# Layer B's memory projection moved into layer A's last pair, and queries projected in halves

## The chip, the cores and the metric

One core of a Trainium2 chip runs the whole kernel. The metric is the device time of one execution in microseconds (us); lower is better. The engines are named as in the profile: PE is TensorE (matmuls), PEld its weight loads, DVE is VectorE, ACT is ScalarE, POOL is GpSimd, SP is SyncE, which issues all DMAs of this kernel.

## What is computed

An encoder of two layers over 1024 tokens of width 1024. Layer A (index 0) uses windowed attention with 12 query heads and 4 key/value heads, layer B (index 1) neighbourhood attention on a 16 x 64 grid with 12 heads. In each layer 4 more heads attend to a memory of 256 rows. Cut to what matters here:

```python
for i in range(DEPTH):                      # DEPTH = 2
    h = rms_norm(x, norm_mix_pre[i])
    m = rms_norm(mem, norm_mem[i])
    mkv = einsum('bmd,de->bme', m, w_mem_kv[i])    # memory keys and values, 256 x 512
    mk, mv = mkv[..., :256], mkv[..., 256:]
    proj = einsum('bsd,de->bse', h, w_in[i])       # queries, keys, values, memory queries
    tok = windowed_gqa(...) if i % 2 == 0 else neighbourhood_attn(...)
    mem_out = memory_attn(qm, mk, mv)
    x = x + rms_norm(concat(tok, mem_out) @ w_out[i], norm_mix_post[i])
    gu = rms_norm(x, norm_ffn_pre[i]) @ w_gu[i]
    x = x + rms_norm((silu(gate) * up) @ w_down[i], norm_ffn_post[i])
```

Memory keys and values of layer B depend on `mem` and on weights alone, so they can be computed at any time before layer B's memory heads.

## The kernel before

Every float32 product is made of three matmuls: each operand is split into a high part (an ACT copy to fp32r) and a low part (a DVE or POOL subtraction), and `mm3` (L91 to L93) adds high x high, high x low and low x high. A weight unit of 128 x 1024 is loaded by `load_raw` (L105, tile `wr`, two buffers) and split by `split_raw` (L115, L116, tiles `wh` and `wl`, three buffers).

**The opening** (L585 on) projects layer A's first values while the rows of x are normed and transposed. Then, for each layer c, it projects key unit c of layer A: the first half (512 tokens) of it, then four transposes of the normed memory rows (L186, split into tiles `mT` by L97 and L98), then the second half, and then that layer's memory keys and values (`memory_kv`): two units of 24 matmuls with 256 columns and two passes of 24 over two units. Layer A's results stay on the chip, but for its second key unit; that one and all of layer B's go to DRAM (`mem_scr`) and are loaded back later (`mem_back`: in layer A with the start of pair 1).

**The attention of a layer** runs over eight pairs of heads in the order 0, 6, 1, 7, 2, 3, 4, 5 (6 and 7 are the memory pairs). A pair has 16 units (8 blocks of 128 tokens, two heads). `heads` writes PE's order by hand: the scores of unit k (L254, L255, tile `pss`), then some matmuls of a filler, then the drains: the transposes of unit k-3 (L282, `pst`) and the weighted values of unit k-5 (L292, `psv`). The filler of a pair is the projection of what the next pair needs, spread evenly over the 16 units; the last pair has none. A query unit (`q_item`) is two halves of 512 tokens, 24 matmuls each into a tile `psg`. Units 0 to 7 of a pair read the first half's tile, units 8 to 15 the second's. The first pair's queries are projected ahead of the pairs.

**A query tile** (`q_tiles`) holds high and low parts of two heads, interleaved over the partitions. In layer A ACT writes the high part (L208), DVE the low part into `ql` (L209, one buffer), and three DMA moves of 64 x 512 (L201) bring the parts to their places; the third move overwrites what the first one reads. In layer B two ACT copies (L215, L216) and two DVE operations (L218) write the parts straight to their places, with no move; layer B's keys are written with twelve moves.

**Other DMAs.** `bias_tiles` (L702) loads the next pair's bias, four DMAs into one of two buffers. `grid_tables` prepares layer B's bias in DRAM in five steps: 8 fills from `maskb` and 16 + 16 from `rpb` into `rpb_d`, then 16 + 8 copies from `rpb_d` to `bias_d` (all L372). One step is begun with each of pairs 0, 1, 2, 3, 4. The scheduler is free to place them on SP's queue. `attn_d` (L657) stores a pair's output when its last unit is weighted. SP issues in the order of the program; an issue that waits holds up all behind it.

PE's order is fixed by hand (`manual_schedule`); on the other engines a scheduler sets it, in which `high_priority(offset=...)` moves an instruction ahead or back.

## Time and profile before

| | us |
|---|---|
| median of 3 runs | 2289.8 |
| lowest, highest | 2287.86, 2291.98 |
| the profiled execution | 2287.94 |
| its span on the page | 2286.2 |
| PE busy in it | 2152.5 (94%) |
| DVE, ACT, POOL busy | 1503.4, 1062.8, 735.5 |

The page's times come from one execution; its span is the time from the first to the last instruction, and 1.7 us lie around it. Times in the rows below are counted from the span's start. A wait is put down to the instruction whose end released it. Layer A's opening takes the first 137.5 us, its pairs stand from there to 373.8, layer B's from 1193.8 to 1507; the rest is the output projections and the feed-forward layers.

### The profile page before, as it was taken

To read this page: it belongs to the slowest core of one execution; us is meant where nothing else is said; L and a number is where in the kernel's file an instruction comes from. 1 tells how busy PE (TensorE), PEld (TensorE's weight loads), DVE (VectorE), ACT (ScalarE), POOL (GpSimd) and SP (SyncE) were. 2 spreads that over 40 slices of the span, in tenths; PEclk is the share of its full clock that TensorE was granted. 3 is DMA by queue.
4 is the path that set the end of the run, shared out by engine and by line. 5 is a ranking of instruction groups with operands and counts; after the bars stand their busy time and mean duration, and the time that the engine had idled before them with its cause. 6 is when DMAs were issued, how large, how long until landed. Compare 5 with 4: busy or idle time off the path is not lost. (4 is left out here: it accounts for less than half of the span.)

```text
span 2286.2 us, 31339 instructions
## 1 busy us (share of the span) xinstructions
PE 2152.5 (94%) x10538; PEld 1783.6 (78%) x10538; DVE 1503.4 (66%) x2621; ACT 1062.8 (46%) x2158; POOL 735.5 (32%) x814
## 2 busy tenths in 40 slices
PE   7789987989999999999899999989899999999986
PEld 6678775868888888787788898868688888888865
DVE  5358775578677775556657765765887777755556
ACT  5458885453323332444447765764432333324333
POOL 3336663242333331011115433433334333311012
PEclk9899998999999999999999999999999999999998
DMA  6343344314545453866442322432255555436665
GB/s 218 81 112 89 91 135 105 114 56 159 197 162 182 167 184 108 297 193 211 156 130 70 98 70 77 133 104 104 74 180 184 175 172 180 154 130 223 192 208 168
DMA packets 152600, 333.88 MB, mean 146 GB/s; under 512 B 24791, under 2 KB 47191, under 8 KB 152440
## 3 DMA queue, kind: packets, MB, share of 16 engines
q1 hardware_dynamic: 152440, 331.88, 45.7%
q8 instruction: 84, 1.38, 0.3%
q14 instruction: 76, 0.62, 0.1%
HBM read 226.96 MB, written 92.93 MB: 140 GB/s over the span
## 5 line engine op out<-in xcount | busy, mean ns | idle before, releaser
L944 DVE TENSOR_TENSOR zt<-acc,zt 128x512 f32<-128x512 f32 x300 | 204.6, 686 | 148.8 <-PE acc L93 146.9
L1089 DVE TENSOR_TENSOR dl<-draw,dh 128x1024 fp32r<-128x1024 f32 x146 | 187.0, 1288 | 164.7 <-ACT dh L1087 164.1
L274 POOL TENSOR_TENSOR sn<-sn,st 128x384 f32<-128x384 f32 (+1 forms) x256 | 189.0, 740 | 237.5 <-DVE st L273 199.6
L1087 ACT ACTIVATE dh<-draw 128x1024 fp32r<-128x1024 f32 x146 | 153.9, 1059 | 219.8 <-PE acc L93 141.4
L92 PE MATMUL acc<-dl,dh 128*128 128x512 f32 x584 | 230.6, 395 | 15.8 <-DVE dl L1089 15.8
L93 PE MATMUL acc<-dh,dl 128*128 128x512 f32 x584 | 229.0, 392 | 0.0
L91 PE MATMUL acc<-dh 128*128 128x512 f32 x584 | 225.2, 391 | 1.9 <-ACT dh L1087 1.7
L887 ACT ACTIVATE gh<-zt 128x512 fp32r<-128x512 f32 x168 | 104.3, 628 | 167.2 <-PE acc L92 146.7
L963 POOL TENSOR_TENSOR tw<-tw 128x512 f32<-128x512 f32 x88 | 132.6, 1507 | 120.0 <-DMA tw<-in_wts 114.2
L116 DVE TENSOR_TENSOR wl<-wr,wh 128x1024 fp32r<-128x1024 f32 x88 | 112.8, 1282 | 87.7 <-ACT wh L115 86.0
L1144 POOL TENSOR_TENSOR tt<-tt,g 128x512 f32<-128x512 f32 x32 | 52.9, 1668 | 365.2 <-ACT junk L1143 365.2
L115 ACT ACTIVATE wh<-wr 128x1024 fp32r<-128x1024 f32 x100 | 105.6, 1056 | 119.7 <-DMA wr<-in_wts 85.2
L940 ACT ACTIVATE zt<-zt 128x512 f32<-128x512 f32 x84 | 53.1, 632 | 225.3 <-DVE zt L944 225.3
L963 POOL TENSOR_TENSOR zt<-zt 128x512 f32<-128x512 f32 x66 | 91.4, 1385 | 205.6 <-DVE zt L941 202.2
L92 PE MATMUL psg<-hL,wh 128*128 128x512 f32 x384 | 153.7, 400 | 0.0
L91 PE MATMUL psg<-hH,wh 128*128 128x512 f32 x384 | 153.5, 400 | 0.0
L93 PE MATMUL psg<-hH,wl 128*128 128x512 f32 x384 | 153.4, 399 | 0.0
L292 PE MATMUL psv<-PT,v 128*128 128x256 f32 x656 | 142.2, 317 | 5.2 <-DVE attn L652 3.6
L98 DVE TENSOR_TENSOR PT<-pst,PT 128x384 fp32r<-128x384 f32 (+1 forms) x256 | 126.7, 495 | 28.5 <-ACT PT L97 24.6
L92 PEld LDWEIGHTS acc<-dl,dh 128*128 128x128 f32 x584 | 110.6, 189 | 43.7 <-DVE dl L1089 21.1
L272 ACT ACTIVATE sn<-sn,st 128x385 f32<-128x385 f32 (+3 forms) x192 | 113.0, 589 | 63.7 <-DVE st L269 56.4
L889 DVE TENSOR_TENSOR gl<-zt,gh 128x512 fp32r<-128x512 f32 x168 | 130.1, 776 | 8.1 <-ACT gh L887 8.0
(218 smaller groups left out, 5965.5 us busy)
## 6 DMA issues: line engine op xcount, KB each, us to landing
wr<-in_wts SPq DMA_DIRECT2D x146, 512.0 KB
draw<-both_d SPq DMA_DIRECT2D x88, 512.0 KB
both_d<-zt SPq DMA_DIRECT2D x88, 256.0 KB
tw<-in_wts SPq DMA_DIRECT2D x44, 512.0 KB
both_d<-tw SPq DMA_DIRECT2D x44, 512.0 KB
act_d<-zt SPq DMA_DIRECT2D x66, 256.0 KB
draw<-act_d SPq DMA_DIRECT2D x66, 256.0 KB
draw<-in_wts SPq DMA_DIRECT2D x66, 256.0 KB
```

Source lines behind the costliest of these rows:

```text
L91: nc.tensor.matmul(ps, lh, rh, start=start, stop=False)
L92: nc.tensor.matmul(ps, lh, rl, start=False, stop=False)
L93: nc.tensor.matmul(ps, ll, rh, start=False, stop=stop)
L98: nc.vector.tensor_tensor(ol, ps, oh.bitcast(F32), ALU.subtract)
L272: nc.scalar.activation(sn[:, :m], sn[:, :m], AF.Exp, bias=nm, scale=-1.0, accum_out=ssum)
L274: nc.gpsimd.tensor_tensor(sf, sf, rinv.broadcast_to([P, n]), ALU.mult)
L292: nc.tensor.matmul(pv[:, j % 2], pair.v(self.lo + c)[:, pair.vh + hh], self.PT[:, c], start=c == 0, stop=c == nk - 1)
L889: nc.vector.tensor_tensor(lo, src, h.bitcast(F32), ALU.subtract)
L944: nc.vector.tensor_tensor(o, a, b, ALU.add)
L963: nc.gpsimd.tensor_tensor(o, a, b, ALU.subtract)
L1087: nc.scalar.activation(h, raw, AF.Copy)
L1089: eng.tensor_tensor(lo, raw, h.bitcast(F32), ALU.subtract)
```

## The change

Layer B's memory rows are still normed and transposed in the opening, but the four `mT` tiles go to DRAM (`mt_d`), are loaded back in layer A's pair 4 into a key buffer that has come free, and are projected as the filler of layer A's last pair (5). In the opening, two steps of the key unit's second half (6 matmuls) now stand behind each transpose of the memory rows.

Queries become two items of half the cost. The first half of a pair's queries is in the filler of the pair before, at its end; the second half is in the filler of the pair itself, at its start, and has to be done by unit 4. Ahead of the first pair only its first half is projected. The tile without moves (`apart`) is used in layer A's first and last token pairs (0 and 5) and in all of layer B; in layer A's other pairs the three moves stay. The DMAs of `grid_tables` are kept in program order with the others that are so marked. Weights are loaded further ahead.

```diff
-    def proj_T(unit, src, n, dst):
+    def proj_T(unit, src, n, dst, start=0):
-        for c0 in range(0, n, HALF):
+        for c0 in range(start, n, HALF):
...
-    def q_tiles(p, ps, w):
+    def q_tiles(p, ps, w, apart):
         t = p.tile([P, 2, HALF], F32R, name="q", tag="q", bufs=4)
-        if windowed:
+        if not apart:
...
                 i = at[0]
                 at[0] += 1
-                load(i)
-                load(i + 1)
+                for k in range(i, i + 3):
+                    load(k)
+                    if k > i and items[k:k + 1] and items[k][3] is None:
+                        break
                 yield from items[i][1](loaded[i])
...
+            due = [sum(it[2] for it in its if it[3] is not None and it[3] <= n) for n in range(16)]
...
-                    while done < cost * (2 * n + part + 1) / (2 * len(units)):
+                    while done < max(cost * (2 * n + part + 1) / (2 * len(units)), due[n]):
                         done += next(fill)
...
         def go(out, in_):
-            return lambda: dma.dma_start(out=out, in_=in_)
+            return lambda: tc.keep_in_program_order(dma.dma_start(out=out, in_=in_))
...
+    mt_d = dpool.tile([2, 2, P, D], F32, name="mt_d")
...
-    def q_item(u, keep):
-        def steps(unit):
+    def q_items(u, keep, apart):
+        loaded = []
+        def load():
+            if not loaded:
+                loaded.append(load_unit(u))
+            return loaded[0]
+        def steps(half):
             def put(c0, w, ps):
-                with tc.high_priority(offset=-LATER):
-                    keep(c0 // HALF, q_tiles(a1, ps, w))
-            return proj_T(unit, src_h, S, put)
-        return (lambda: load_unit(u)), steps, 16 * 1024
+                with tc.high_priority(offset=0 if half else -LATER):
+                    keep(half, q_tiles(a1, ps, w, apart))
+            return lambda unit: proj_T(unit, src_h, (half + 1) * HALF, put, half * HALF)
+        return [(load, steps(0), 8 * 1024, None), (load, steps(1), 8 * 1024, 4)]
...
                 split_ps(pt, *(mT[k][b][:, :, i * P:(i + 1) * P] for k in range(2)))
+                for _ in range(2):
+                    next(pump)
...
+            mT = memory(rows, gen)
+            if c:
+                for k in range(2):
+                    for b in range(2):
+                        dma.dma_start(out=mt_d[k, b], in_=mT[k][b].rearrange("p c t -> p (c t)").bitcast(F32))
             run(gen)
-            memory_kv(c, src)
+            if c == 0:
+                src = mem_src(mT)
+                for it in memory_items(0, lambda: src, lambda: npool.tile([P, 256], F32, name="mraw", bufs=2)):
+                    now(it)
+                bias_tables(npool)
...
-                return units, [q_item(U_A + p, keep_q(p))]
+                return units, [], q_items(U_A + p, keep_q(p), p in (order[0], order[7]))
...
+                k, v = kv_items(p)
+                qs = q_items(U_B + p, keep_q(p), True)
+                return units, k, [qs[0], *v, qs[1]]
...
-        for it in needs[order[0]]:
+        for it in needs[order[0]][0]:
             now(it)
-        groups = [(units_by[c], needs[n] if n is not None else []) for c, n in zip(order, order[1:] + [None])]
+        groups = [(units_by[c], needs[c][1] + (needs[n][0] if n is not None else []))
+                  for c, n in zip(order, order[1:] + [None])]
+        if windowed:
+            back = []
+            def reload(then=units_by[order[6]]):
+                t = a1.tile([P, 4, S], F32R, name="mTk", tag="k", bufs=2)
+                for k in range(2):
+                    for b in range(2):
+                        dma.dma_start(out=t[:, 2 * k + b].bitcast(F32), in_=mt_d[k, b])
...
+            groups[6] = reload, groups[6][1]
+            groups[7] = groups[7][0], groups[7][1] + memory_items(
+                1, lambda: mem_src(back), lambda: at2.tile([P, 3 * P + 8], F32, name="sn", bufs=TURN + SNX)[:, :256])
```

What this makes of the engines' orders at three places follows. On PE, at the border of layer A's pairs 0 and 6, before (`q_1162` is pair 0's second half, `q_1333` pair 6's first, made from another `psg` eight units earlier; `psg_1367` is pair 6's second half):

```order
L254 MATMUL pss_1537<-k6_575,q_1162 128x256
L255 MATMUL pss_1537<-k6_575,q_1162 128x256
L91 MATMUL psg_1367<-hH_104,wh8_1173 128x512
L92 MATMUL psg_1367<-hL_105,wh8_1173 128x512
L93 MATMUL psg_1367<-hH_104,wl8_1174 128x512
L282 MATMUL pst_1558<-ident_63,sn_1465 128x128 x3
L292 MATMUL psv_1509<-PT_1502,v_412 128x256
L292 MATMUL psv_1509<-PT_1502,v_464 128x256
L292 MATMUL psv_1509<-PT_1502,v_516 128x256
L254 MATMUL pss_1573<-mk_705,q_1333 128x256
```

The same border on PE after (`psg_1200` is pair 6's first half, from which `q_1383` is made):

```order
L254 MATMUL pss_1370<-k6_576,q_1106 128x256
L255 MATMUL pss_1370<-k6_576,q_1106 128x256
L91 MATMUL psg_1200<-hH_105,wh8_1031 128x512
L92 MATMUL psg_1200<-hL_106,wh8_1031 128x512
L93 MATMUL psg_1200<-hH_105,wl8_1032 128x512
L282 MATMUL pst_1391<-ident_63,sn_1298 128x128 x3
L292 MATMUL psv_1342<-PT_1335,v_413 128x256
L292 MATMUL psv_1342<-PT_1335,v_465 128x256
L292 MATMUL psv_1342<-PT_1335,v_517 128x256
L254 MATMUL pss_1406<-mk_706,q_1383 128x256
```

The half whose last matmuls stand just ahead of the border was the one for units 8 to 15; it is now the one that the next instruction behind the drains reads.

On SP, at the border of layer A's pairs 2 and 3, before (`q_3034` and `q_3251` are pair 3's halves, `attn_3051` pair 2's output, `bias_3274` the bias of pair 4):

```order
L201 DMA q_2804<-ql_2805 64x512
L201 DMA q_3034<-q_3034 64x512
L372 DMA bias_d_77<-rpb_d1_76 12x16x384
L201 DMA q_3034<-ql_3035 64x512 x2
L372 DMA bias_d_77<-rpb_d1_76 12x16x384
L702 DMA bias_3274<-vec_d_74 32x2x384 x4
L201 DMA q_3251<-q_3251 64x512
L201 DMA q_3251<-ql_3252 64x512
L657 DMA attn_d0_1093<-attn_3051 128x1024
L201 DMA q_3251<-ql_3252 64x512
```

The same place on SP after (`q_3084` and `q_3251` are pair 3's halves, `mTk` the reloaded memory rows):

```order
L685 DMA attn_d0_962<-attn_2453 128x1024
L201 DMA q_2798<-ql_2799 64x512
L105 DMA wr37_4158<-in_wts 128x1024
L817 DMA mTk_3560<-mt_d_85 128x1024
L730 DMA bias_3107<-vec_d_74 32x2x384 x4
L376 DMA bias_d_77<-rpb_d0_75 12x16x128 x16
L201 DMA q_3084<-q_3084 64x512
L201 DMA q_3084<-ql_3085 64x512
L817 DMA mTk_3560<-mt_d_85 128x1024
L201 DMA q_3084<-ql_3085 64x512
L817 DMA mTk_3560<-mt_d_85 128x1024 x2
L201 DMA q_3251<-q_3251 64x512
```

The copies to `bias_d`, one or two between other DMAs before, now stand as a block of sixteen behind the bias loads and ahead of the moves of pair 3's first half. A block of eight stands likewise ahead of pair 4's.

On PE in the opening, before, from the last matmuls of key unit 1 on:

```order
L91 MATMUL psg_919<-hH_104,wh7_849 128x512
L92 MATMUL psg_919<-hL_105,wh7_849 128x512
L93 MATMUL psg_919<-hH_104,wl7_850 128x512
L91 MATMUL psg_958<-mT_887,wh36_954 128x256
L92 MATMUL psg_958<-mT_889,wh36_954 128x256
L93 MATMUL psg_958<-mT_887,wl36_955 128x256
```

The same place on PE after:

```order
L91 MATMUL psg_899<-hH_105,wh7_850 128x512
L92 MATMUL psg_899<-hL_106,wh7_850 128x512
L93 MATMUL psg_899<-hH_105,wl7_851 128x512
L91 MATMUL psg_974<-hH_105,wh0_970 128x512
L92 MATMUL psg_974<-hL_106,wh0_970 128x512
L93 MATMUL psg_974<-hH_105,wl0_971 128x512
```

Where layer B's memory units (weights 36 to 39) stood, pair 0's first query half follows the key unit at once.

## Rows read from the trace of the kernel before

**Rows 1.** The page's first line.

```profile
span 2286.2 us, 31339 instructions
```

**Rows 2.** Windows: stretch, then busy us (instructions) by engine, PEclk, DMA share, GB/s.

```profile
0.00:137.40 137.40, 103.20 (x626) 91.35 (x626) 55.47 (x87) 61.52 (x102) 38.47 (x34) 0.92 0.57 155
137.40:333.20 195.80, 185.47 (x1108) 158.32 (x1109) 153.17 (x483) 160.18 (x455) 129.46 (x239) 0.97 0.33 92
333.20:373.80 40.60, 25.81 (x142) 19.31 (x140) 26.63 (x85) 29.04 (x82) 24.62 (x46) 0.87 0.43 95
...
1475.60:1507.00 31.40, 21.76 (x141) 17.11 (x140) 26.26 (x83) 28.73 (x80) 20.85 (x29) 1.00 0.36 110
```

**Rows 3.** Waits of PE from 48 to 138: us, times, longest.

```profile
PE pss L254 <- DMA q<-ql: 7.2, 1, 7.2
PE pst L186 <- DVE mT L98: 4.7, 3, 2.4
PE psg L91 <- ACT wh L115: 4.3, 1, 4.3
...
PE psg L92 <- POOL wl L116: 1.8, 1, 1.8
```

**Rows 4.** Waits of PE from 140 to 374.

```profile
PE pss L254 <- DMA q<-ql: 12.6, 4, 6.4
PE pst L282 <- POOL sn L274: 3.7, 7, 0.8
```

**Rows 5.** Timeline of PE at 302: start, us, instruction, shape, count [idle before].

```profile
301.92 0.39 PE L93 MATMUL psg<-hH,wl 128*128 128x512 f32 x1
...
302.83 0.28 PE L254 MATMUL pss<-k,q 128*128 128x256 f32 x1
```

**Rows 6.** Timeline of ACT and of DVE there.

```profile
302.35 0.60 ACT L208 ACTIVATE q<-psg 128x512 fp32r<-128x512 f32 x1 [0.35 <-PE psg L93]
...
302.98 0.69 DVE L209 SCALAR_TENSOR_TENSOR ql<-psg,q 128x512 fp32r<-128x512 f32 x1
```

**Rows 7.** Windows with 512 columns alone, then with 256 columns alone.

```profile
550.00:600.00 50.00, 50.00 (x218) 40.52 (x217) 37.79 (x53) 14.36 (x23) 16.39 (x12) 1.00 0.54 185
...
1163.00:1172.00 9.00, 9.00 (x76) 8.91 (x76) 3.28 (x7) 3.31 (x8) 0.00 (x0) 1.00 0.43 124
```

**Rows 8.** Window at half clock around layer A's first scores.

```profile
133.70:140.60 6.90, 3.11 (x10) 2.68 (x11) 1.84 (x6) 0.61 (x3) 0.61 (x1) 0.51 0.51 134
```

**Rows 9.** Timeline of SP: first and third move of a query tile.

```profile
149.53 0.52 SPq L201 DMA_DIRECT2D q<-q  x1
...
151.85 0.47 SPq L201 DMA_DIRECT2D q<-ql  x1
```

**Rows 10.** Timeline of SP: the third move for pair 2's second half.

```profile
254.36 0.47 SPq L201 DMA_DIRECT2D q<-ql  x1
```

**Rows 11.** Timeline of PE: the scores that waited for it (unit 8).

```profile
257.54 0.41 PE L254 MATMUL pss<-k,q 128*128 128x384 f32 x1 [2.09 <-DMA q<-ql]
```

**Rows 12.** Timeline of SP at the border of pairs 3 and 4.

```profile
303.01 1.73 SPq L702 DMA_DIRECT2D bias<-vec_d  x4
304.78 1.54 SPq L372 DMA_DIRECT2D bias_d<-rpb_d  x2
```

**Rows 13.** Line 372 on SP: ns min/median/max of an issue, first and last start.

```profile
L372 SPq DMA_DIRECT2D rpb_d<-in_rpb x32: 737/757/1404, 53.6 to 141.9; - x32
L372 SPq DMA_DIRECT2D bias_d<-rpb_d x24: 723/765/791, 142.7 to 305.6; - x24
```

**Rows 14.** Timeline of SP: moves of the memory keys.

```profile
194.54 2.45 SPq L201 DMA_DIRECT2D mk<-mk  x4
```

**Rows 15.** Timeline of SP: the last moves of layer B's first keys.

```profile
1187.37 1.57 SPq L201 DMA_DIRECT2D k<-k  x2
```

**Rows 16.** Timeline of PE: layer B's first scores.

```profile
1193.83 0.28 PE L254 MATMUL pss<-k,q 128*128 128x256 f32 x1
```

More of the change, by code (lines that the diff above doesn't have):

```diff
@@ L513, in steps @@
             return proj_N(units, src_h, NT, put)
[L514 removed]
+        return (lambda: [load_unit(u), load_unit(u + 1)]), steps, 64 * 512, None
     def now(item):
@@ L519, in first_values @@
     def first_values(u, keep, turns):
-        load, steps, _ = v_item(u, keep)
+        load, steps, _, _ = v_item(u, keep)
         gen = steps(load())
@@ L556, in memory_rows, with mem_src, memory @@
         return [norm_rows(npool, raw_tile(mem_in, i), g, 2) for i in range(2)]
-    def memory(rows):
+    def mem_src(mT):
+        return lambda kc, cs: tuple(t[kc // 4][:, kc % 4, cs] for t in mT)
+    def memory(rows, pump):
         mT = [[a1.tile([P, 2, HALF], F32R, name="mT", tag="q", bufs=4).rearrange(
@@ L564, in put, with memory_items @@
                 split_ps(pt, *(mT[k][b][:, :, i * P:(i + 1) * P] for k in range(2)))
+                for _ in range(2):
+                    next(pump)
             turn(pp["psT"], "pst", rows[i], put)
-        return lambda kc, cs: tuple(mT[k][kc // 4][:, kc % 4, cs] for k in range(2))
-    def memory_kv(layer, src):
+        return mT
+    def memory_items(layer, src, raw_tile):
         def keep(k, ps):
             if layer or k == 1:
-                t = npool.tile([P, 256], F32, name="mraw", bufs=2)
+                t = raw_tile()
                 nc.scalar.activation(t, ps, AF.Copy)
@@ L580, in memory_kv @@
         u0 = U_MEM + 4 * layer
+        its = []
         for c in range(2):
-            run(proj_T(load_unit(u0 + c), src, MEM, lambda c0, w, ps, c=c: keep(c, ps)))
-        run(proj_N([load_unit(u0 + 2), load_unit(u0 + 3)], src, 2, lambda i, ps: keep(2 + i, ps)))
+            its.append((lambda c=c: load_unit(u0 + c),
+                        lambda unit, c=c: proj_T(unit, src(), MEM, lambda c0, w, ps: keep(c, ps)), 8 * 512, None))
+        its.append((lambda: [load_unit(u0 + 2), load_unit(u0 + 3)],
+                    lambda units: proj_N(units, src(), 2, lambda i, ps: keep(2 + i, ps)), 16 * 512, None))
+        return its
     with tc.manual_schedule(engines=PE_ONLY):
@@ L588, in build @@
             rows = memory_rows(c)
-            load, steps, _ = k_item(U_A + 6 + c, lambda t, c=c: kts.__setitem__(c, t))
+            load, steps, _, _ = k_item(U_A + 6 + c, lambda t, c=c: kts.__setitem__(c, t))
             lk[0] = LKS
@@ L767, in build @@
         for p in range(6):
-            units_by[p], needs[p] = group(p)
+            units_by[p], first, rest = group(p)
+            needs[p] = first + rest[:-1], rest[-1:]
         for m in range(2):
```

21 lines of the change are left out of this document (10 added, 11 removed).

## The prediction

> **What bounds the kernel now.** I read the span first [rows 1], then busy time by stretch [rows 2]. In layer A's first seven pairs TensorE (PE) is busy 185.47 of 195.8 us, ScalarE (ACT) 160.18: these pairs are bound by TensorE, and a microsecond in which it waits there is a microsecond of the result. The opening before them (137.4 us) has only 103.20 us of TensorE, at a granted clock of 0.92; layer A's last pair 25.81 of 40.6; layer B's last pair 21.76 of 31.4. These three stretches have room, and the change takes work from the first and puts it into the other two. Next I read what ended TensorE's waits in the opening [rows 3]: moves of the query tile (7.2), transposes of the memory rows (4.7), weights of the memory units (4.3 and 1.8). In the pairs, 12.6 us of waits for the query moves, in four places [rows 4], stand against some 3.7 for the next cause. So what has to be read closely is the way from a projected query half to the scores that use it. At the border of pairs 3 and 4 [rows 5, 6] the last matmul of a half ends at 302.31; ACT copies it from 302.35 (0.60), VectorE (DVE) takes the low part from 302.98 (0.69), and the next pair's scores start at 302.83 without a wait. They can, because the half just finished is the second one, needed eight units later.
>
> **The opening.** Removed: layer B's memory projection, 24 + 24 + 48 = 96 matmuls of 256 columns at 9.00/76 = 0.118 us [rows 7], 11.4 us; and one query half, 24 matmuls of 512 columns at 50/218 = 0.229 [rows 7], 5.5 us. The 4.7 us at the transposes go: 6 matmuls of the key unit (1.4 us) now stand behind each. The 4.3 and 1.8 for the memory units' weights go with the units. The 7.2 at the first scores becomes the way of a tile without moves, ACT 0.60, then twice DVE 0.69 (durations of the full-width form, [rows 6]), 2.0 and with a queue 2.5: 4.7 less. Half clock: after the 7.2 us wait TensorE had a granted clock of 0.51 (its lower level, 1.2 GHz) for 6.9 us and was busy 3.11 of them [rows 8]; with the waits go two such stretches and a part of a third, 4 us. Against it I set 2.5 us of new waits (0 to 6), since the first query weights and the key splits now follow each other closely on VectorE. The four stores of the memory rows and the bias loads behind them I put at nothing: the query half's 5.5 us cover them; uncovered they cost some 3. Sum: -11.4 - 5.5 - 4.7 - 6.1 - 4.7 - 4 + 2.5 = **-34** (-28 to -39).
>
> **The pair borders of layer A.** This is the term that decides. Each group's filler now holds its own second query half first and the next pair's first half last; the order shows the last matmuls of that half directly ahead of the old pair's last drains, and then scores that read it. Only pairs 0 and 5 use tiles without moves; the other six borders need three moves. By the rows of the border above: ACT done 302.95, first move issued 303.0. The third move overwrites what the first one reads, so it waits for that one's landing: 2.3 us from issue to issue (149.53 to 151.85, [rows 9]); I take 2.4. From the third move's issue to the scores: 254.36 to 257.54, 3.2 us [rows 10, 11]. Scores at 303.0 + 2.4 + 3.15 = 308.5 instead of 302.83: **5.7 us** of wait, with nothing on TensorE that could run in it. Bounds: 4.5 (moves that meet an empty queue) and 8.
>
> SyncE's queue (SP) adds to it, since it issues in order. Into pair 3 four bias loads and sixteen copies to bias_d stand ahead of the first move, and the bias loads wait for the old pair's last softmax: in the trace they start at 303.01 and take 1.73, and the copies follow at 304.78, 1.54 for two [rows 12]; the median copy is 0.765 over 24, never under 0.72 [rows 13]. Sixteen at a step of 0.80 (0.77 and the gap of 0.04 that stands between these rows): the first move at 317.6, scores at 323.2, a wait of 20.3. Into pair 4 it is eight copies: 304.78 + 6.4 + 2.4 + 3.15, a wait of 13.9. Into pair 7 one bias load (0.43) comes first: 6.1. Into pair 1 the third move stands behind four moves of the memory keys, and these behind a load and a split: load at 302.7, landed 3.1 later (as a move), ACT and DVE some 0.8, and the four moves 2.45 [rows 14], so scores at 311.8, a wait of 9.0. Into pairs 6 and 2: 5.7 each. Into pair 5, without moves, ACT and DVE of a half tile behind their queues less the drains, 1.2. Sum 5.7 + 9.0 + 6.1 + 5.7 + 20.3 + 13.9 + 1.2 = **+62** (45 to 75).
>
> After six such waits the clock comes back low. 3.11 us of busy time at half clock [rows 8] are at most 1.55 lost; I take 1.2 each, **+7** (0 to 12).
>
> The Trainium skill, DMA: Bandwidth & Descriptors, section Anatomy of one DMA, fits a transfer (issued by GpSimd) as about 2.0 us plus bytes over 436 GB/s. For a move of 128 KB that is 2.3 us by estimate; the trace's 3.2 to the scores is longer, and by the page each of the six borders would be nearly 1 us cheaper.
>
> **Within the pairs.** The second half must be done by unit 4 and is needed at unit 8. Its third move still follows the store of the last pair's output. Three of the four waits there make 12.6 - 6.4, some 2 us each [rows 4]; they stay, at unit 8 of pairs 2 to 4, and I expect the same newly in pairs 6 and 1: **+4** (0 to 10; sixteen rpb copies ahead of pair 7's second half could add 6). Pulling the half forward empties the filler of units 5 to 7, where ACT then leads: **+2** (0 to 8).
>
> **Layer A's last pair** takes 96 matmuls (11.4) and a query half (5.5). From its start to the output projection's first matmul it took 40.6 us with 25.81 busy [rows 2]; with 16.9 more, TensorE alone has 42.7. The wait of 6.4 for moves [rows 4] goes, as its tiles have none. The four weight splits and the three units of the output projection that were loaded ahead now compete there. I take 44: **+3.5** (0 to 9).
>
> **Layer B.** Its first query half saves 5.5 us ahead of the pairs, but the last two key moves are issued from 1187.37 for 1.57 us and scores began at 1193.83 [rows 15, 16]; with 3.15 from the last issue the keys are there at 1191.6, so the start gains 2, not 5.5. Its borders have no moves: ACT 0.60 and DVE 0.69 [rows 6] less the drains, 1 us at the five borders where the query half comes last, +5. Two emptied stretches, +1. The last pair has 9.6 us idle and gets 5.5 of matmuls in a burst, ACT and DVE over a microsecond each: +3. Sum **+7** (0 to 12).
>
> **The sum** on the profiled execution (2287.94, 1.9 under the median of the three): -34 + 62 + 7 + 4 + 2 + 3.5 + 7 = +51.5, **2339 us**.
>
> **Rivals.** (a) The queue is not the price I take it for: the copies cost SP little, and into pairs 3 and 4 there remain the bias loads and the bare wait, 5.7 + 1.7 each. That is 19.4 less, 2320. For it: sixteen in a row do not occur in the trace, and their data are small. Against it: 24 copies and 32 others, none issued in under 0.72. The Trainium skill, same page, section Issuing engines are not separate DMA queues, calls the time to start a DMA usually small beside the transfer; by that rule this rival would hold, and the trace's 0.765 us speaks against it.
>
> (b) **Faster.** The place is the same six borders. If a first half's tile were ready by the end of the drains, nothing would stand against the shorter opening: 2339 - 62 - 7 = 2270. The point from which it decides is a mean of (69 - 51.5)/6 = 2.9 us for one of the six, clock included: below it the change gains. For it: the waits in the pairs are mostly about 2 us. Against it: those follow a tile finished eight units before, and the chain of ACT, DVE and two moves in series is over 5 us [rows 5, 6, 9 to 11].
>
> (c) **Slower still.** The moves do not land in 3.2 us behind the copies. The longest wait now is 6.4 [rows 4], where loads stood ahead in the queue. Twice 6 us more, and pair 7's second half late by 6: 2357 and up.
>
> **How the numbers follow.** The forecast 0.72, (a) 0.14, (b) 0.05, (c) 0.09. The forecast's own bounds do not all fall together; its range is 2318 to 2357. To hold 8 in 10 with part of (a) and (c) I give 2312 to 2360. What a measurement can tell from no change is about 0.2%, 2285.2 to 2294.4. Faster 0.04, the same 0.03, slower 0.93.
>
> **What would show it.** The first scores at 103 to 104 us instead of 137.5. At each of layer A's borders a wait of the scores for query moves: 5 to 9 us into 6, 1, 7 and 2, about 20 into 3 and 14 into 4; none for moves into 5. On SP sixteen copies to bias_d ahead of pair 3's first move. In the last pair TensorE busy over 40 us, without a wait over 2. In layer B waits of about 1 us. I am wrong if the waits into 3 and 4 are like the others (rival a), or if all are under 3 (rival b).

## The result and the profile after

The changed kernel takes 2385.7 us (median; 2380.6 to 2388.3) against 2289.7 beside it: a ratio of 1.0416, 95% interval 1.0396 to 1.0436. It is slower, as forecast, but by 96 us where 49 over the median were forecast, and outside the range of 2312 to 2360. The profiled execution has this span (answer to [rows 1]):

```profile
span 2384.9 us, 31287 instructions
```

The stretches of [rows 2] in the changed kernel (stretch, then busy us and instructions by engine, PEclk, DMA share, GB/s): opening, layer A's first seven pairs, its last pair, all that lies between, layer B's first seven pairs, its last pair.

```profile
0.00:102.01 102.01, 81.61 (x506) 72.26 (x506) 55.40 (x87) 54.87 (x93) 28.53 (x30) 0.97 0.58 171
102.01:392.45 290.44, 200.99 (x1108) 171.26 (x1108) 161.62 (x491) 166.52 (x463) 134.72 (x242) 0.86 0.28 76
392.45:441.03 48.58, 38.60 (x261) 35.30 (x261) 32.57 (x87) 33.69 (x86) 25.30 (x42) 0.90 0.43 125
441.03:1260.62 819.59, 795.86 (x3548) 649.58 (x3548) 541.20 (x701) 308.31 (x493) 202.81 (x156) 0.98 0.50 166
1260.62:1567.66 307.04, 287.13 (x1733) 252.13 (x1733) 192.84 (x538) 196.47 (x511) 121.01 (x165) 0.97 0.28 76
1567.66:1604.16 36.50, 28.37 (x165) 23.09 (x165) 26.20 (x83) 28.56 (x78) 19.70 (x27) 0.95 0.28 95
```

Layer B's first seven pairs in the kernel before, which [rows 2] leave out:

```profile
1193.83:1475.66 281.83, 277.18 (x1734) 244.84 (x1732) 188.56 (x536) 195.20 (x510) 119.71 (x164) 1.00 0.30 82
```

The opening is 35.4 us shorter. Layer A's seven pairs are 94.6 longer. Read the first busy time of the second row against [rows 2]: the same 1108 matmuls keep TensorE busy 15.5 us longer, at a granted clock of 0.86 where it was 0.97, and TensorE is idle 89.5 us where it was 10. Layer B's seven pairs are 25.2 us longer, 10.0 of that again busy time. The last pairs add 8.0 and 5.1.

What TensorE waited for in layer A's seven pairs, three rows, and in layer B's pairs, two rows (us in sum, times, longest), against [rows 4]:

```profile
PE pss L254 <- DMA q<-ql: 74.4, 12, 21.1
PE pst L282 <- DVE PT L98: 9.2, 10, 2.1
PE pst L282 <- DVE st L273: 1.9, 1, 1.9
...
PE pss L254 <- DVE q L218: 12.7, 5, 2.9
PE pst L282 <- DVE PT L98: 7.2, 4, 2.3
```

The 74.4 us are six borders (5.06 into pair 6, 7.23 into 1, 5.05 into 7, 6.58 into 2, 21.09 into 3, 16.37 into 4) and six waits at unit 8. With 3.13 into pair 5 the borders make 64.5. The border into pair 3 on SP and then the scores on TensorE (start, us, instruction, count):

```profile
286.87 1.73 SPq L730 DMA_DIRECT2D bias<-vec_d  x4
288.64 12.73 SPq L376 DMA_DIRECT2D bias_d<-rpb_d  x16
301.48 0.52 SPq L201 DMA_DIRECT2D q<-q  x1
...
303.88 0.47 SPq L201 DMA_DIRECT2D q<-ql  x1
...
307.85 0.55 PE L254 MATMUL pss<-k,q 128*128 128x256 f32 x1 [21.09 <-DMA q<-ql]
```

Sixteen copies take 12.73 us of SP, a step of 0.80, with no other work of SP between them; the first move stands behind them, the third 2.40 later, and the scores 3.97 behind that.

A border of layer B, into pair 1, in the timeline: TensorE's last projecting matmul and the scores, then ACT, then VectorE.

```profile
1329.47 0.40 PE L93 MATMUL psg<-hH,wl 128*128 128x512 f32 x1
1332.40 0.39 PE L254 MATMUL pss<-k,q 128*128 128x256 f32 x1 [2.53 <-DVE q L218]
...
1330.03 0.38 ACT L679 ACTIVATE pb<-psv 64x256 f32<-64x256 f32 x1
1330.43 0.59 ACT L215 ACTIVATE q<-psg 64x512 fp32r<-64x512 f32 x1
1331.03 0.59 ACT L216 ACTIVATE q<-psg 64x512 fp32r<-64x512 f32 x1
...
1331.66 1.41 DVE L218 SCALAR_TENSOR_TENSOR q<-psg,q 64x512 fp32r<-64x512 f32 x2 [0.80 <-ACT q L216]
```

The window behind it:

```profile
1332.70:1336.10 3.40, 3.40 (x13) 2.89 (x12) 2.10 (x8) 1.77 (x6) 0.00 (x0) 0.50 0.17 41
```

ACT first finishes the old pair's output, then makes both copies, and VectorE starts only behind the second copy. The window is the price that no list of waits shows: TensorE is busy without a break, 3.40 of 3.40 us, but the granted clock is 0.50, its lower level, 1.2 GHz.

### The profile page after: what moved, and what is told of

It is laid out like the page before. It is cut to its first block, busy times and chain, and to the rows that moved or that the text cites. A ratio compares the mean times of both kernels' runs of the same rounds, so it can differ in the third digit from the quotient of the medians.

```text
span 2384.9 us, 31287 instructions
## 1 busy us (share of the span) xinstructions
PE 2177.1 (91%) x10538; PEld 1806.8 (76%) x10538; DVE 1522.9 (64%) x2629; ACT 1068.7 (45%) x2162; POOL 730.8 (31%) x810
## 4 chain that ended last, share of the span: by engine, by line
PE 73%; DVE 7%; DMA 7%; ACT 5%; issue 3%; POOL 3%; SPq 2%; POOLq 0%; ACTq 0%; DVEq 0%
PE acc L92 18%; PE acc L93 17%; PE acc L91 17%; PE psg L91 4%; PE psg L92 4%; PE psg L93 4%; PE psv L292 2%; PE pst L282 2%; PE pss L254 1%; DMA wr<-in_wts 1%; DMA q<-ql 1%; PE pss L255 1%; SPq L376 1%; DMA draw<-in_wts 1%; POOL zh L871 1%
## 5 line engine op out<-in xcount | busy, mean ns | idle before, releaser
L92 PE MATMUL acc<-dl,dh 128*128 128x512 f32 x584 | 232.2, 398 | 15.3 <-DVE dl L1138 13.2
L272 ACT ACTIVATE sn<-sn,st 128x385 f32<-128x385 f32 (+3 forms) x192 | 113.0, 588 | 119.8 <-DVE st L269 108.7
L1193 POOL TENSOR_TENSOR tt<-tt,g 128x512 f32<-128x512 f32 x32 | 51.5, 1620 | 371.7 <-ACT junk L1192 371.7
L116 DVE TENSOR_TENSOR wl<-wr,wh 128x1024 fp32r<-128x1024 f32 x92 | 118.6, 1290 | 66.4 <-ACT wh L115 64.8
L91 PE MATMUL psg<-hH,wh 128*128 128x512 f32 x384 | 158.5, 413 | 0.4 <-DVE v L98 0.4
L292 PE MATMUL psv<-PT,v 128*128 128x256 f32 x656 | 147.2, 326 | 7.7 <-DVE attn L680 4.7
L282 PE MATMUL pst<-ident,sn 128*128 128x128 f32 x656 | 120.4, 285 | 22.7 <-DVE PT L98 18.6
```

The costliest lines, as they stand in the source:

```text
L91: nc.tensor.matmul(ps, lh, rh, start=start, stop=False)
L92: nc.tensor.matmul(ps, lh, rl, start=False, stop=False)
L116: b = low[0].tensor_tensor(lo, raw, h.bitcast(F32), ALU.subtract)
L282: nc.tensor.transpose(pt[:, c], self.sn[:, c * P:(c + 1) * P], ident)
L292: nc.tensor.matmul(pv[:, j % 2], pair.v(self.lo + c)[:, pair.vh + hh], self.PT[:, c], start=c == 0, stop=c == nk - 1)
```

## The experiments

Two names help: a *border* is the change from one pair to the next, and *the kernel without moves* is the second run. A ratio is to the kernel before, run beside it. The parts of the change come first, then the causes.

### e1_free_grid: the copies to bias_d out of the way

```diff
-            return lambda: tc.keep_in_program_order(dma.dma_start(out=out, in_=in_))
+            return lambda: dma.dma_start(out=out, in_=in_)
```

> The changed kernel with one thing undone: the copies that build layer B's bias table are no longer kept in program order, so SP issues the sixteen and the eight copies to bias_d spread over pairs 0 to 2 instead of directly ahead of the first query move into pairs 3 and 4. Theory (issue time on SP is what makes these two borders long): the waits of 21.09 and 16.37 us become 5 to 8 each, the other borders stay at 5 to 7.3, and the half-clock time behind the two long waits shrinks by some 4 us of busy time; 2385.7 - 15 - 10 - 3 = 2358 us (2350 to 2365). Rival (the copies cost SP little, and the two borders are long because the transfers themselves meet other traffic): the two waits stay over 13, 2380 us or more.

Measured: 2359.4 us, ratio 1.0300 (1.0283 to 1.0318). SP into pair 3 (timeline):

```profile
288.38 1.73 SPq L730 DMA_DIRECT2D bias<-vec_d  x4
290.21 0.47 SPq L201 DMA_DIRECT2D q<-q  x1
```

The waits in the seven pairs:

```profile
PE pss L254 <- DMA q<-ql: 51.9, 12, 7.8
```

The first move now follows the bias loads at once. The wait into pair 3 is 7.78 us and into pair 4 6.85; those into 6, 1, 7 and 2 stay at 4.6 to 7.3. So the time falls by 26 of the 96 us with one line of the diff that has nothing to do with queries or memory (the line frees all five steps of `grid_tables`, not the two with the copies alone). The theory holds for the waits. That the time comes within 1.4 us of its number is partly luck: the seven pairs are 18.1 us shorter in the profile, since the waits for moves fall by 22.5, but busy time rises by 2.8 where some 4 less were expected, and the waits at units 6 and 7 rise by 2.4. The other 9 us lie elsewhere, 3.9 of them between layer A's last pair and layer B's first scores, a stretch that took between 812 and 820 us in the profiles of the versions with halves.

### e2_no_moves: no DMA between a half and its scores

```diff
-                return units, [], q_items(U_A + p, keep_q(p), p in (order[0], order[7]))
+                return units, [], q_items(U_A + p, keep_q(p), True)
...
-            qs = q_items(um + m, keep_q(6 + m), not windowed)
+            qs = q_items(um + m, keep_q(6 + m), True)
```

> The changed kernel, but all of layer A's query tiles are written in the form without moves (ACT twice and VectorE twice on 64 partitions), so that no DMA stands between a query half and its scores. Theory (the price of a border is the chain of moves and its queue): the seven borders fall from 64.5 us in sum to 1.2 to 3 us each, about 17, like layer B's; the waits at unit 8 (13 us) go to under 4; the half clock in these pairs costs about half of its 15 us; 2385.7 - 48 - 9 - 7 = 2322 us (2312 to 2335). The time that remains over the kernel before (about 32) is then not the moves. Rival (the bound is the way of the projected half over ACT and VectorE, with their queues): with twice the instructions there the borders stay at 5 us or more, and ACT, busy 82% of these pairs, starts to lead; 2345 us or more.

Measured: 2341.0 us, ratio 1.0221 (1.0198 to 1.0244), between the two. The window of the seven pairs, and one of 3.4 us behind the border into pair 1:

```profile
101.91:349.83 247.92, 204.13 (x1109) 175.53 (x1109) 168.63 (x503) 173.21 (x475) 130.97 (x242) 0.88 0.23 66
...
169.00:172.40 3.40, 3.40 (x15) 3.00 (x13) 2.29 (x8) 2.22 (x8) 0.60 (x4) 0.50 0.27 66
```

The waits in the seven pairs:

```profile
PE pss L254 <- DVE q L218: 19.9, 6, 3.7
PE pst L282 <- DVE PT L98: 13.4, 6, 2.3
```

Borders of 3.2 to 4.0 us remain, 24.8 in sum, where 17 were expected, and the busy time stays 18.7 us over the kernel before. (One of the six waits in the first line is the 2.48 us ahead of pair 0's scores; two borders stand outside it, 3.33 into pair 7, put down to the bias loads, and 4.02 into pair 5, where the window ends.) The moves and their queue are worth 45 us together, 42.5 of them in these pairs. Layer A's last pair is 5.9 us longer than in the changed kernel (54.5 us; 53.5 to 56.8 in all later runs without moves); why was not tried. Three things beside the moves stand up: short waits at the borders, waits of 1.9 to 2.3 us at unit 6, and half clock behind most of both. The next three runs of this kernel take one each.

### e3_memory_alone and e4_halves_alone: the two parts apart

In e3 (the core of its edit) the queries are whole again:

```diff
-                return units, [], q_items(U_A + p, keep_q(p), p in (order[0], order[7]))
+                return units, q_items(U_A + p, keep_q(p), p in (order[0], order[7])), []
...
-            needs[p] = first + rest[:-1], rest[-1:]
+            needs[p] = first, rest
```

In e4 layer B's memory is projected in the opening; the stores, the reload and the filler of the last pair go:

```diff
-            if c == 0:
-                src = mem_src(mT)
-                for it in memory_items(0, lambda: src, lambda: npool.tile([P, 256], F32, name="mraw", bufs=2)):
-                    now(it)
+            src = mem_src(mT)
+            for it in memory_items(c, lambda: src, lambda: npool.tile([P, 256], F32, name="mraw", bufs=2)):
+                now(it)
```

> One part of the change alone: layer B's memory projection in layer A's last pair, but the queries whole again, projected in the pair ahead as in the kernel before (the copies to bias_d stay in program order). Theory (the memory's move gains, the halves lose): the opening ends some 30 us earlier (a query half, 5.5, is in it again), layer A's last pair is 0 to 4 us longer, and no pair border waits for moves of the half just projected. The sixteen copies now stand ahead of the moves that unit 8 of pair 3 needs, a wait of some 6 us there; 2289.7 - 30 + 3 + 6 = 2269 us (2258 to 2282). Rival (the move of the memory itself brings a loss, because layer A's last pair and layer B's start have no room for it): 2290 us or more.

> The other part alone: queries in halves, the second within the pair's own units, as in the changed kernel, but layer B's memory projected in the opening as before (no stores and no reload of the memory rows). Theory (the two parts add up): the changed kernel less what the memory's move gains, 30 less 3 to 9; 2385.7 + 24 = 2410 us (2400 to 2420), with border waits in layer A as in the changed kernel. Rival (the parts interact: the reload and the stores of the memory rows, and the 16 KB weights ahead, are what loads SP and the borders): waits at the borders under 50 us in sum and a time under 2385.

Measured: e3 2270.9 us, ratio 0.9917 (0.9901 to 0.9932); e4 2397.4, ratio 1.0472 (1.0443 to 1.0500). The memory's move gains 19 us and the halves alone lose 108; 89 in sum against the 96 of both. The time of e4 lies 2.6 us under its range. e3 is not the memory's move in every respect alone: the change's smaller parts stay in it, the tiles without moves in pairs 0 and 5, the key matmuls between the transposes and the weights loaded further ahead. Of e3 the windows of the opening and of layer A's last pair, then SP into pair 3 in the timeline; of e4 the same two windows.

```profile
0.00:105.15 105.15, 85.27 (x531) 75.06 (x531) 56.10 (x87) 54.93 (x93) 28.60 (x30) 0.98 0.60 172
...
315.01:355.37 40.36, 32.07 (x238) 29.64 (x237) 32.16 (x91) 34.48 (x91) 26.69 (x45) 0.94 0.50 151
```

```profile
248.47 12.71 SPq L376 DMA_DIRECT2D bias_d<-rpb_d  x16
261.28 0.52 SPq L201 DMA_DIRECT2D q<-q  x1
```

```profile
0.00:122.80 122.80, 96.27 (x603) 86.35 (x603) 56.66 (x87) 60.46 (x101) 38.94 (x34) 0.93 0.52 152
...
424.62:463.51 38.89, 29.85 (x165) 24.29 (x165) 27.27 (x83) 29.11 (x78) 21.97 (x42) 0.91 0.39 89
```

Layer A's last pair has room for either part: 40.4 us with the memory alone, 38.9 with the half alone, 40.6 before [rows 2]. With both it takes 48.6. In e3 no border waits for the half just finished, but the order of the queue costs there too: the border into pair 6 waits 6.16 us for moves, unit 8 of pair 3, with the sixteen copies ahead of its moves, 7.43, and unit 8 of pair 4 3.09. That is worth a run of its own, e8.

### e5_no_moves_busy: the waits stay, TensorE works in them

```diff
             run(fill)
+            if len(line) < 8 * 2 * NT:
+                ps = pp["psG"].tile([P, HALF], F32, name="psg")
+                for _ in range(spare):
+                    nc.tensor.matmul(ps, hH[:, 0, :P], hH[:, 0, :HALF], start=True, stop=True)
```

`spare` is 12 in layer A and 8 in layer B; the rest is the kernel without moves.

> The kernel without moves (layer A's query tiles all written without moves), with matmuls of no use put at every pair border, behind the last matmul of the half and ahead of the scores: 12 of 512 columns in layer A (2.75 us at 0.229), 8 in layer B (1.8 us), less than the waits of 3.2 to 4.0 and 2.2 to 2.9 there. The waits stay, but TensorE works in them. Theory (a wait of some 3 us costs a second time, since half clock follows it): of the half-clock stretches in layer A's pairs about half begin at a border, the others behind the waits of 2.3 us at unit 7, which stay; so of some 18.7 us of busy time lost there 8 come back, in layer B 4 of 8.5; 2341 - 12 = 2329 us (2322 to 2336). Rival (the half clock follows from something else, or is hidden by waits elsewhere): 2341 us or up to 5 more.

Measured: 2326.0 us, ratio 1.0176 (1.0153 to 1.0199), 15 us less than e2 (10 by the ratios, whose intervals just meet) with 140 more matmuls. The seven pairs, and 3.4 us behind the border into pair 1, to hold against the last row of e2:

```profile
101.90:336.67 234.77, 210.28 (x1192) 179.52 (x1192) 168.31 (x503) 173.39 (x475) 131.13 (x242) 0.94 0.24 70
164.60:168.00 3.40, 3.40 (x21) 3.02 (x22) 2.39 (x7) 2.24 (x7) 0.62 (x4) 1.00 0.20 52
```

84 of the 1192 matmuls are the useless ones, 84 x 0.229 = 19.2 us; the useful ones take 191.0 where they took 204.1. The stretch is 13.2 us shorter, just as much. All half clock behind the borders is gone; it remains behind six waits at unit 6. So the half clock is a price of its own: about 2 us for each border of 3.5.

### e6_no_moves_first and e7_no_moves_spread: the two short waits

```diff
-                with tc.high_priority(offset=0 if half else -LATER):
+                with tc.high_priority(offset=0):
```

> The kernel without moves, with one thing changed: ACT's and VectorE's writes of a first query half no longer rank behind later work (an offset of -60 in the priority, now 0, as the second half has it), so that on ACT the second copy stands ahead of the transposes' copy and the two copies of the old pair's output, and on VectorE the two subtractions follow at once. Theory (what makes a border without moves 3.2 to 4.0 us long is the queue of the old pair's drains on ACT and VectorE): a border becomes ACT 0.60 + VectorE 0.70 + some 0.1 behind the last matmul, 1.5 us in layer A and 1.3 to 1.5 in layer B; 7 x 1.9 + 4 of clock in layer A, 6 x 1.1 + 2 in layer B, 2341 - 26 = 2315 us (2308 to 2328). Rival (the queue is full either way, and what is overtaken is late next: the drains that stand behind now hold up the new pair's first units): the borders shrink and the waits come back within three units, 2335 us or more.

Measured: 2327.9 us, ratio 1.0184 (1.0164 to 1.0204), 13 us less than e2 (8 by the ratios), half of what was expected. ACT and VectorE at the border into pair 3 (the half's last matmul ends at 261.9):

```profile
261.97 0.59 ACT L215 ACTIVATE q<-psg 64x512 fp32r<-64x512 f32 x1
262.97 0.51 ACT L272 ACTIVATE sn<-sn,st 128x257 f32<-128x257 f32 x1 [0.41 <-DVE st L269]
...
263.60 0.59 ACT L216 ACTIVATE q<-psg 64x512 fp32r<-64x512 f32 x1
...
264.22 1.41 DVE L218 SCALAR_TENSOR_TENSOR q<-psg,q 64x512 fp32r<-64x512 f32 x2 [0.45 <-ACT q L216]
```

The old pair's drains stand behind now, and the borders fall from 24.8 to 18.3 us in layer A (the one into pair 5 stays, at 4.12). Two things were not in the theory: an exponential (L272) still runs between the two copies, and VectorE's first subtraction waits for the second copy. Whether the order copy, subtraction, copy, subtraction would spare that was not tried. The rival fails: the waits did not come back later.

```diff
-        return [(load, steps(0), 8 * 1024, None), (load, steps(1), 8 * 1024, 4)]
+        return [(load, steps(0), 8 * 1024, None), (load, steps(1), 8 * 1024, 7)]
```

> The kernel without moves, with the second query half due by unit 7 instead of unit 4, so that its matmuls are spread over units 0 to 7 and units 5 to 7 keep filler. Theory (the waits of 1.9 to 2.3 us at unit 6 or 7 of each pair come from the empty filler there, and half clock follows them): seven such waits, 15.3 us in sum, go, about 1 us each comes at unit 8, where the half is now only just ready, and half of the 18.7 us of lost clock comes back; 2341 - 15 + 7 - 8 = 2325 us (2316 to 2334). Rival (these waits are ACT's and VectorE's own work at that point of a pair, not missing filler): they stay or move by a unit, 2338 us or more.

Measured: 2336.1 us, ratio 1.0219 (1.0201 to 1.0237). That is 5 us under e2, but at the same ratio, so no gain in time is shown, where 16 were expected. The waits of the seven pairs:

```profile
PE pss L254 <- DVE q L218: 41.2, 14, 3.7
```

The theory is right on the cause and wrong on the price. With filler in units 5 to 7 the waits for `PT` are gone, all of them. But the seven waits at unit 8 are 1.9 to 3.1 us each, 18.5 in sum, not 7: a half that is finished just ahead of its use pays there much as at a border (3.1 to 3.9 in this run).

### e9_early_first and e10_no_moves_early: the halves finished in time

In layer A the first half is due by unit 12 (e9, on e1) or 13 (e10, on e6) of the pair ahead. Both also keep the loading of weights as it was.

```diff
-        return [(load, steps(0), 8 * 1024, None), (load, steps(1), 8 * 1024, 4)]
+        return [(load, steps(0), 8 * 1024, 12 if u < U_B else None), (load, steps(1), 8 * 1024, 4)]
```

> The changed kernel with the copies free of the program order, and in layer A the next pair's first query half due by unit 12 of the pair ahead instead of at its end, so that some four units (6.5 us) lie between its last matmul and the border. Theory (the halves lose because a half is needed the moment it is finished, not because there are two of them): the border waits, 41 us in sum with the copies free, go to under 6 (into pair 1, behind the moves of the memory keys, some 3 stay); units 13 to 15 now have no filler, a wait of 2.3 us in each of seven pairs, 16; half clock gives back some 4. 2359.4 - 36 + 14 - 4 = 2333 us (2322 to 2345). Rival (the same filler, packed into two bursts, leaves ACT to lead in between, and what the border gives is lost in the units): 2350 us or more.

> The kernel without moves, the first query half written without the rank behind later work and, in layer A, due by unit 13 of the pair ahead. Theory (time between a half's last matmul and its use is what was missing; ACT and VectorE need 3.4 us, two units and a half are 4): layer A's borders, 24.8 us in sum without moves, go to under 3; units 14 and 15 lose their filler, 1 us in each of seven pairs, 7; half clock gives back 6; layer B as with the first halves ranked first, 2 less. 2341.0 - 22 + 7 - 6 - 2 = 2318 us (2306 to 2328), still over the kernel before, since layer B's borders and clock (21) and the last pair of layer A (14) stay. Rival (the units cannot take it): 2328 us, as with the rank alone, or more.

Measured: e9 2336.5 us, ratio 1.0198 (1.0178 to 1.0219); e10 2318.6, ratio 1.0124 (1.0109 to 1.0139). Both times lie in their ranges, but in both the parts missed and made up for each other. In e9 the borders keep 12.7 us, not under 6, and units 13 to 15 lose about 1, not 16: the 14.7 us below are nearly all at units 6 and 7, where e1 has 13.5. In e10 the borders go as expected; units 14 and 15 lose 13.2 us, not 7, and the busy time falls by 13.4 against e2, not 6. The waits in the seven pairs, of e9 and then of e10, and the window of e10's:

```profile
PE pss L254 <- DMA q<-ql: 24.6, 12, 3.6
PE pst L282 <- DVE PT L98: 14.7, 14, 2.3
```

```profile
PE pst L282 <- DVE st L273: 15.1, 8, 2.0
PE pst L282 <- DVE PT L98: 13.8, 6, 2.3
```

```profile
101.43:326.13 224.70, 190.74 (x1109) 165.07 (x1110) 165.59 (x500) 171.25 (x471) 128.73 (x238) 0.94 0.26 73
```

In e10 no border from pair 6 on waits at all, and the stretch is still 29 us over the 195.8 of [rows 2]. In place of the borders stand 28.9 us of waits in units that lost their filler: 15.7 at unit 6, where e2 had 15.3 (13.4 and 1.9), and 13.2 at unit 15, in seven waits of 1.9 to 2.0. The empty filler alone does not make those seven, since e9 has none in units 13 to 15 either. In e10 ACT and VectorE write the next pair's tile there: at the end of pair 1 their two copies and two subtractions run ahead of the exponential and the reciprocal that TensorE then waits for. Whether that is the cause was not tried. This is the fastest version with halves that was run, and it is slower than the kernel before.

### e8_memory_free_grid: what is left if the halves go

This is e3 with the copies free as in e1; the smaller parts named there stay in it.

> The memory's move alone, queries whole as in the kernel before, and the copies that build layer B's bias table free of the program order again, as in the kernel before. Theory (in the run of the memory's move alone the waits of 7.43 and 3.09 us at unit 8 of pairs 3 and 4 come from the copies on SP): both become about 2 or nothing, with the half clock behind them; 2270.9 - 8 - 3 = 2260 us (2253 to 2266), 1.3% under the kernel before. Rival (the copies, spread, stand ahead of other moves, those into pair 6 or of pair 1's memory keys): 2268 us or more.

Measured: 2254.3 us, ratio 0.9852 (0.9832 to 0.9873): 1.5% under the kernel before, 131 us under the changed one. The opening, the seven pairs and the last pair:

```profile
0.00:105.83 105.83, 85.70 (x530) 75.50 (x531) 55.94 (x87) 54.91 (x93) 28.52 (x30) 0.97 0.61 180
105.83:296.74 190.91, 181.98 (x1110) 154.09 (x1109) 153.84 (x485) 162.26 (x459) 129.26 (x239) 1.00 0.37 108
296.74:336.71 39.97, 32.66 (x239) 29.84 (x237) 32.86 (x92) 34.80 (x91) 26.44 (x46) 0.93 0.50 152
```

The opening gives 31.6 us, the pairs another 4.9, and the last pair takes 96 more matmuls at no cost in time. Not all of that is the memory's move: with the tiles without moves in pairs 0 and 5 the waits of 7.2 us at the first scores [rows 3] and of 6.4 in the last pair [rows 4] are gone, and the second makes room for the 96 matmuls. What each part is worth was not measured. Of e3's three waits for moves one is left, 1.84 us at unit 8 of pair 4.

### e11_memory_early and e12_best_memory_early: layer A's last pair

Both make the memory projection due by unit 11 of the last pair, e11 in the changed kernel, e12 in e8 (`memory_items`, both places).

```diff
-                        lambda unit, c=c: proj_T(unit, src(), MEM, lambda c0, w, ps: keep(c, ps)), 8 * 512, None))
+                        lambda unit, c=c: proj_T(unit, src(), MEM, lambda c0, w, ps: keep(c, ps)), 8 * 512, 11))
```

> The changed kernel with one number: in layer A's last pair the filler with layer B's memory projection is due by unit 11 instead of the pair's end, so that its last stores, and the weight loads among which they stand on SP, come some 4 units (7 us) earlier. In the changed kernel the loads of the attention output (ao) were issued at 435.52, behind them, and the output projection's first matmul waited 4.77 us. Theory (the last pair's excess is this queue on SP): the loads go out 3 to 5 us earlier, the wait falls to under 1, the half clock behind it goes with it, and units 12 to 15 lose their filler, 1 us: the stretch from the last pair's start to that matmul falls from 48.6 to 44 to 46 us; 2385.7 - 4 = 2382 us. Rival (the loads wait for something at the pair's end itself, such as the place of their tile): issue and wait stay as they are, 48 us or more there, 2386 us.

> The same number in the kernel with the memory's move alone and free copies (2254.3 us), whose first matmul of the output projection waited 2.66 us. Theory: the wait goes, 1 us comes back in units 12 to 15; 2254.3 - 2 = 2252 us (2249 to 2255). Rival: 2254 us or more, and the wait of 2.66 stays.

Measured: e11 2384.8 us, ratio 1.0422 (1.0399 to 1.0446); e12 2255.4, ratio 0.9858 (0.9837 to 0.9878): neither moves its kernel. SP and the output projection's first matmul, in the changed kernel and in e11:

```profile
435.52 0.97 SPq L882 DMA_DIRECT2D ao<-attn_d  x2
...
441.03 0.79 PE L91 MATMUL acc<-wh,aoH 128*128 128x512 f32 x1 [4.77 <-ACT aoH L892]
```

```profile
431.97 1.05 SPq L882 DMA_DIRECT2D ao<-attn_d  x2
...
443.85 0.50 PE L91 MATMUL acc<-wh,aoH 128*128 128x512 f32 x1 [1.92 <-ACT aoH L892]
```

Counted from the pair's start the loads go out at 35.1 us where it was 43.1, and the wait falls by 2.9, so the rival, a wait for the pair's end itself, does not hold. But TensorE's busy time in the stretch rises by 1.6 while its idle time falls by 3.2, and the stretch only goes from 48.6 to 47.0. In e12 the wait is 1.92 where it was 2.66, and the time is the same. The queue is a small part of the last pair's excess of 8.0.

## Why the prediction missed, step by step

| term | forecast | measured |
|---|---|---|
| opening | -34 | -35.4 |
| layer A's borders | +62 | +64.5 |
| clock in layer A's pairs | +7 | +15.5 |
| waits at unit 8 | +4 | +6.8 (74.4 - 61.4 = 13.0, less the 12.6 - 6.4 of [rows 4]) |
| emptied filler in layer A | +2 | +11.1 (9.2 + 1.9) |
| other waits in layer A's pairs | 0 | -3.3 (the remainder) |
| layer A's last pair | +3.5 | +8.0 |
| layer B's start | -2 | -0.4 (TensorE waits 2.0 for weights there) |
| layer B's pairs | +6 | +25.2 (clock 10.0, borders 12.7, the rest 2.5) |
| layer B's last pair | +3 | +5.1 |
| after layer B | 0 | +1.6 |
| sum | +51.5 | +98.7 |

**What was right.** The mechanism, and the two largest terms. The opening came out as summed. The borders came out nearer in sum than one by one: those into 4, 5, 2 and 3 were longer than forecast, by 2.5, 1.9, 0.9 and 0.8 us, those into 1, 7 and 6 shorter, by 1.8, 1.1 and 0.6, so a part of the agreement is luck. (Into pair 1 the forecast's own pieces add up to 312.2 and a wait of 9.4, not to 311.8 and 9.0.) At the border into pair 3 the order of the queue, the step of 0.80, the 2.4 us between first and third move and the length (20.3 forecast, 21.09 measured) all hold; only the last piece, issue to scores, was 3.97 where 3.15 was taken from [rows 10, 11]. Rival (a) is refuted by e1: the copies cost SP its 0.8 us each, and 26 us go when they move away. The Trainium skill, DMA: Bandwidth & Descriptors, section Issuing engines are not separate DMA queues, calls the time to start a DMA usually small beside the transfer. That gives no measure of this wait: what holds the move up is SP's time to start the copies, 0.80 us each, sixteen times. How long the transfers themselves take no run shows, so whether the start is small beside them stays open; the 0.765 us that the prediction sets against the rule does not settle it. Rival (b) did not occur, since no border with moves was under 5 us; that halves ready in time would have gained was wrong too, as e10 shows: layer A's borders are at nothing there, and the whole is 29 us over the kernel before.

**Step that failed first: the clock.** I took 1.2 us lost behind each of six borders, from a window in which TensorE seemed only half busy [rows 8], and nothing in layer B. Measured are 15.5 and 10.0. The first is the figure of one execution: e1, e11 and e4, with the same matmuls in these pairs, are busy there for 203.8, 207.5 and 211.1 us, 18 to 26 over the kernel before. Two things were mis-sized. The window of [rows 8] begins at 133.7, and the wait in it ends only at 137.49; behind it TensorE is busy throughout, and a stretch at half clock that is full of matmuls loses half its length, 1.7 of 3.4 us. And mostly a wait of 2 to 3 us is followed by such a stretch as well, not only a long one: in the first seven pairs of both layers of the changed kernel this holds, within 5 us, for 9 of 10 such waits, among them all of layer B's borders that wait. e5 shows it as a cause: the borders' waits kept, the half clock taken away, 13.2 us back in layer A's seven pairs. The kernel before shows it too. There the waits at unit 8 of pairs 3 and 4 (2.38 and 1.80 us) end at 287.6 and 317.9; the stretches around and behind them:

```profile
287.30:290.70 3.40, 3.07 (x10) 2.71 (x11) 1.77 (x5) 0.78 (x3) 0.77 (x2) 0.50 0.67 163
318.00:321.50 3.50, 3.50 (x13) 3.10 (x14) 1.71 (x5) 1.61 (x4) 1.62 (x4) 0.51 0.97 321
```

It is not a rule: behind the third wait at unit 8 there, 2.09 us in pair 2 [rows 11], and behind the 3.13 us into pair 5 of the changed kernel, the clock stays at 1.00 for the 3.4 us that follow. What decides between the two these runs do not show.

**Step that failed second: a border without moves.** The prediction says of layer B "ACT 0.60 and DVE 0.69 [rows 6] less the drains, 1 us", and 1.2 for pair 5 of layer A. Measured are 2.2 to 2.9 and 3.13. For the very same form of tile, at the first scores of the opening, I had allowed "ACT 0.60, then twice DVE 0.69 ... with a queue 2.5", and 2.48 was measured there. The tile takes two copies and two subtractions, and the old pair's output stands ahead of them on both engines. e6 shows the queue's part (24.8 to 18.3 us in layer A).

**Step that failed third: the emptied filler.** I put +2 on "ACT then leads" in units 5 to 7, with 0 to 8 as bounds and no row behind it. Measured are 11.1 in layer A. e7 shows the cause (filler spread, waits gone), and e10 that it is no detail: with due times at both ends of a pair the same filler comes in bursts, and the units without it wait 28.9 us in sum, 13.2 of them with a second cause that is not settled.

**Layer A's last pair.** It was read as "TensorE alone has 42.7" and 44 in sum, so 1.3 us idle. Measured are 38.6 busy and 10.0 idle. Each part alone fits: the stretch was 25.8 busy and 14.8 idle before [rows 2], and is 32.1 and 8.3 with the memory alone (e3), 29.9 and 9.0 with the half alone (e4). Both parts went into the same idle time, and at least 6.8 us of it (e11) did not give way in any run. Of the 10.0, 4.77 are the wait for the attention output, in small part by the queue on SP (e11); what holds the rest was not tried.

**The range.** These terms erred in one direction, and the bounds had been narrowed on the ground that they do not all fall together. All but the last pair have one thing in common, and I treated them as separate: they are short waits in stretches that TensorE bounds, and most of these bring half clock with them.

## What to carry to other kernels

A step that is moved to just ahead of its use pays the whole way of its result, once per use; count every copy, subtraction and DMA on that way, and what stands ahead of each in its queue. In a stretch bound by TensorE, price a wait of 2 to 3 us at its length and up to about 2 us more for the clock, and look in the trace before for windows at the lower level behind waits of that size. A gain and a loss that come in one diff can be parted: without the halves, and with the copies' order left as it was, the rest of the change makes the kernel 1.5% faster.

## What the runs showed of the hardware

- Matmuls of no use in a wait pay: 84 of them, 19.2 us of TensorE, made layer A's seven pairs 13.2 us shorter (e2 to e5, one profile of each), since the granted clock behind the borders stayed at 1.00 instead of 0.50.
- A wait of 2.53 us, with TensorE busy at a granted clock of 1.00 ahead of it, was followed by 3.4 us at 0.50 (layer B, into pair 1); in the kernel before, waits of 2.38 and 1.80 us were followed by 0.50 and 0.51 as well, and one of 2.09 us by 1.00.
- Sixteen small DMAs in a row hold SP for 12.73 us; two moves issued one behind the landing of the other stand 2.40 apart in the changed kernel, 2.3 in the kernel before [rows 9].
